# In-projection and pool projection of a hybrid encoder block: token tiles, or feature-major seven-product passes over 1024 tokens

## The chip, the cores and the metric

The kernel runs on one core of a Trainium2 chip. A core has five engines that run side by side and wait for one another by semaphores: TensorE (PE; its weight loads are listed as PEld), VectorE (DVE), ScalarE (ACT), GpSimd (POOL) and SyncE (SP). SP does no arithmetic here: it issues DMA transfers in the order in which the program has them, and an issue that has to wait holds back those behind it. The metric is the device time of the whole kernel in microseconds (us).

## What is computed

One layer of an encoder block over 2048 tokens of width 1024, in float32. Only the first part of it is touched by the change:

```python
xn = rmsnorm(h, g_mix[l])
z = jnp.einsum('bsd,dc->bsc', xn, w_in[l])      # 512 q, 512 k, 512 v, 512 pool columns, 8 gate columns
q = rmsnorm(head_split(q, FOX_HEADS, FOX_HEAD_DIM), g_q_fox[l])     # 8 heads of 64; k alike
fox = forgetting_attention(q, k, v, f_logit)    # causal, with cumulated log-sigmoid gates
pool = multiscale_pool(p_in, w_pool[l], pool_scale[l])  # trailing means over 2, 4, 8, 16 frames, minus the frame, then a map per group
h = h + jnp.einsum('bsc,cd->bsd', jnp.concatenate([fox, pool], axis=-1), w_out[l])
```

Behind it come cross-attention to 256 memory tokens, whose keys and values are a projection of the normed memory, and a gated feed-forward part (FFN). Products have to be nearly as exact as float32.

## The kernel before

**Exactness.** A float32 value is used as a pair: hi is the value rounded to the type fp32r (an ACT copy), lo is what is left (a DVE subtraction, `sub_hi`, L54). `split` (L179) makes the pair, `split_gain` (L175) does so with a factor per partition. A product is then three matmuls (`mm3`, L57): hi by hi, hi by lo and lo by hi. Matmuls on plain float32 data also occur, for small sums; each of them leaves two records in the trace.

**Order.** Where `in_order` is opened, PE and the engines named in it follow the program's order (all of them in the first two stages below, PE alone in the pool stage, PE, DVE and ACT in attention); a planner orders the others by its own costs and by what is ready.

**Stages around the change**, each with its lines:

- Memory keys and values first (L212 to L310): 256 memory tokens by 1024 columns, 96 matmuls of 512 columns, while the in-projection's weights are loaded and split. They go to DRAM (`mkvd`).
- In-projection (L313 to L447): 16 tiles of 128 tokens. For each, the tile of x transposed is the stationary operand, and the 1544 columns of q, k, v and gates are the moving one, in four banks of 386 columns: 4 x 8 x 3 matmuls a tile (`project`, L316). The weights stay on chip as pairs. The row factor of the norm comes from plain float32 sums (`token_sums`, L197) and POOL's `pow` (`rsqrt`, L64), and is applied when a bank is emptied (`scaled`, L324). `normed_heads` (L336) and `split_heads` (L355) norm q and k and split them, `to_heads` (L367) turns them with PE transposes, 16 a tile, to one row per feature, and stores them in DRAM (`qkT`).
- Pool stage (L467 to L628): eight blocks of 256 tokens. `project_p` (L379) has the weights as the stationary operand and 256 columns of x as the moving one, 96 matmuls a block. `windows` (L496) makes the trailing means by doubling sums, all four groups at once; `pooled` (L536) maps them, 12 matmuls a block. `out_sums` (L548) makes weight sums for the output projection on POOL, `cumulated` (L565) the sums of the gates. `load_head` (L456) fetches head 0.
- Attention (from L673): 8 heads by 4 blocks of 512 tokens. `score_items` (L693) issues the scores into `sps`; DVE takes their minima and ACT their exponentials.
- Output projection, cross-attention and FFN. The output projection and the FFN already multiply 2 x 2 blocks of operands with seven products in place of eight: sums and differences of weight blocks are made by DVE or POOL (`weight_ops`, L981; `down_sums`, L1445; `act_sums`, L1466), each block is split, and each product is 12 matmuls of 512 columns into a bank (`product`, L1476). `gate_up` (L1481) is called the gate and up stage below.

## Time and profile before

| what | us |
|---|---|
| median of three timed runs | 2585.02 (2584.59 to 2588.13) |
| the profiled execution, its span from the first to the last instruction | 2586.7 |
| first score of attention issued, in that execution | 460.2 |
| PE busy up to there | 440.13 |

The page gives no other time for the profiled execution than its span, so the span stands for it; it lies 1.7 above the median of the timed runs. In the lines that follow, a row of a timeline has start, length, engine, line of the program, operation, output and inputs, and in brackets how long its engine sat idle before it and what ended that. A row of a group has the number of instructions, their busy time, and the mean length of one in nanoseconds. A row of windows has the window, its length, the busy time of PE, PEld, DVE, ACT and POOL with their numbers of instructions, the granted clock of PE, the DMA share and GB/s.

### The profile page before, as it was taken

The page shows a single profiled execution, that of the slowest core. Times are in us where ns is not written, and L with a number is a line of the kernel's source. Part 1 is how long each engine was busy: PE and PEld are TensorE (multiplying, and loading weights), DVE is VectorE, ACT ScalarE, POOL GpSimd, SP SyncE. Part 2 cuts the span into 40 slices and gives each one's busy share as a digit, 9 for nine tenths or more (in the row PEclk, how much of TensorE's full clock was granted, in tenths as well). Part 3 has the DMA queues.
Part 4 walks back from the last instruction along what each step waited for, and adds up shares of the span by engine and source line. Part 5 has one row for each costly group of instructions (what it writes and reads, how often), then busy time and mean ns, then how long its engine had stood idle before and what let it go on. Part 6 is the DMA issues. An engine that isn't in the chain of part 4 may idle for free.

```text
span 2586.7 us, 37147 instructions
## 1 busy us (share of the span) xinstructions
PE 2522.3 (98%) x13037; PEld 2169.7 (84%) x13037; DVE 1740.9 (67%) x2955; ACT 1286.9 (50%) x2444; POOL 892.2 (34%) x1185
## 2 busy tenths in 40 slices
PE   8999989999999899999999999999999999999998
PEld 7999989788888687788878888888888888888887
DVE  6444477899998755545877778756766666665554
ACT  6454443788889523555643433334543333333443
POOL 3343255445555522344425545430001222222000
PEclk9999999999999999999999999999999999999999
DMA  6443476644543545122464545447773332325665
GB/s 242 127 131 106 127 220 213 175 123 123 152 121 95 171 161 212 70 87 89 177 215 179 187 171 195 147 159 268 247 261 123 113 112 102 127 98 181 230 215 184
DMA packets 223434, 416.13 MB, mean 161 GB/s; under 512 B 26128, under 2 KB 113936, under 8 KB 212496
## 3 DMA queue, kind: packets, MB, share of 16 engines
q1 hardware_dynamic: 190800, 307.84, 37.2%
q0 software_dynamic: 32448, 105.93, 10.6%
q8 instruction: 102, 1.67, 0.3%
q14 instruction: 84, 0.69, 0.1%
HBM read 280.39 MB, written 133.30 MB: 160 GB/s over the span
## 4 chain that ended last, share of the span: by engine, by line
PE 46%; issue 8%; DVE 2%; DMA 2%; ACT 1%; POOL 1%; SPq 0%; POOLq 0%; DVEq 0%; ACTq 0%
PE bk L60 13%; PE bk L62 13%; PE bk L61 13%; PE mmps L60 2%; PE mmps L62 2%; PE mmps L61 2%; PE tp L896 1%; DMA graw<-in_w_gu_dram 1%; DVE ww L55 1%; DVE t L991 0%; DMA xraw<-hTd 0%; POOL out_dram L1578 0%; ACT mq L1069 0%; DMA hTd<-hst 0%; DVE ms L1073 0%
## 5 line engine op out<-in xcount | busy, mean ns | idle before, releaser
L55 DVE TENSOR_TENSOR ww<-draw,ww 128x512 fp32r<-128x512 f32 x308 | 205.3, 703 | 156.5 <-ACT ww L181 155.8
L181 ACT CAST ww<-draw 128x512 fp32r<-128x512 f32 x308 | 179.4, 620 | 219.7 <-PE bk L62 179.2
L55 DVE TENSOR_TENSOR ww<-graw,ww 128x512 fp32r<-128x512 f32 x220 | 179.1, 821 | 107.4 <-ACT ww L181 107.0
L61 PE MATMUL bk<-ww,ww 128*128 128x512 f32 x616 | 239.9, 389 | 0.0
L62 PE MATMUL bk<-ww,ww 128*128 128x512 f32 x616 | 239.8, 389 | 0.0
L60 PE MATMUL bk<-ww,ww 128*128 128x512 f32 x616 | 239.8, 389 | 0.0
L181 ACT CAST ww<-graw 128x512 fp32r<-128x512 f32 x220 | 135.7, 621 | 181.5 <-PE bk L62 158.1
L55 DVE TENSOR_TENSOR pl<-tp,ph 128x512 fp32r<-128x512 f32 (+3 forms) x296 | 176.9, 599 | 27.5 <-ACT ph L809 25.4
L728 ACT ACTIVATE s<-s,mx 128x1024 f32<-128x1024 f32 (+2 forms) x192 | 173.7, 905 | 5.4 <-DVE mx L722 4.5
L793 PE MATMUL tp<-ident,s 128*128 128x128 f32 x1088 | 171.6, 274 | 4.7 <-DVE pl L55 4.3
L60 PE MATMUL zps<-wh,xhi 128*128 128x386 f32 x512 | 175.8, 343 | 0.1
L61 PE MATMUL zps<-wl,xhi 128*128 128x386 f32 x512 | 173.7, 339 | 0.0
L62 PE MATMUL zps<-wh,xl 128*128 128x386 f32 x512 | 173.4, 339 | 0.0
L809 ACT CAST ph<-tp 128x512 fp32r<-128x512 f32 (+3 forms) x296 | 148.5, 513 | 35.9 <-PE tp L793 30.3
L793 PEld LDWEIGHTS tp<-ident,s 128*128 128x128 f32 x1088 | 134.1, 141 | 32.5 <-DVE pl L55 7.7
L1578 POOL DMA_DIRECT2D out_dram<-o x32 | 17.3, 541 | 382.6 <-DVE o L1575 381.6
L62 PE MATMUL bk<-qs,ww 128*128 128x512 f32 x352 | 137.3, 390 | 1.0 <-DVE ww L55 1.0
L60 PE MATMUL bk<-qs,ww 128*128 128x512 f32 x352 | 138.0, 392 | 0.3 <-ACT s L1497 0.3
L61 PE MATMUL bk<-kh,ww 128*128 128x512 f32 x352 | 137.1, 389 | 0.0
L61 PE MATMUL bk<-cb,ww 128*128 128x512 f32 x352 | 137.0, 389 | 0.0
L60 PE MATMUL bk<-kl,ww 128*128 128x512 f32 x352 | 137.0, 389 | 0.0
L62 PE MATMUL bk<-kl,ww 128*128 128x512 f32 x352 | 137.0, 389 | 0.0
(607 smaller groups left out, 7373.4 us busy)
## 6 DMA issues: line engine op xcount, KB each, us to landing
graw<-in_w_gu_dram SPq DMA_DIRECT2D x44, 1024.0 KB, 5.4
draw<-in_w_down_dram SPq DMA_DIRECT2D x66, 256.0 KB, 4.4
xl<-in_xT_dram SPq DMA_DIRECT2D x64, 256.0 KB, 4.9
qkT<-st SPq DMA_DIRECT2D x64, 256.0 KB, 2.7
wdr<-in_w_down_dram SPq DMA_DIRECT2D x22, 512.0 KB, 4.3
vd<-cb SPq DMA_DIRECT2D x16, 512.0 KB, 3.3
qs<-qkT SPq DMA_DIRECT2D x8, 1024.0 KB, 6.8
kh<-qkT SPq DMA_DIRECT2D x16, 512.0 KB, 7.9
```

Source lines behind the costliest of these rows:

```text
L55: (eng or dve).tensor_tensor(out=lo, in0=src, in1=f(hi), op=ALU.subtract)
L60: pe.matmul(ps, lhsT=sh, rhs=mh, start=first, stop=False, skip_group_check=goes_on)
L61: pe.matmul(ps, lhsT=sh, rhs=ml, start=False, stop=False, skip_group_check=goes_on)
L62: pe.matmul(ps, lhsT=sl, rhs=mh, start=False, stop=last, skip_group_check=goes_on)
L181: act.copy(hi, raw)
L728: act.activation(s[:, sl], s[:, sl], AF.Exp, bias=ng, scale=-1.0, accum_out=l[:, q, g:g + 1])
L793: pe.transpose(tp[:, q * P:(q + 1) * P], unit["rows"][q][:, j * P:(j + 1) * P], ident[:])
L809: act.copy(ph[:, sl], tp[:, sl])
L896: pe.transpose(tp[:, e_], src[:, q + e_], ident[:])
L1578: pool.dma_start(out[rows_, cs], o)
```

## The change

The memory stage, the in-projection and the pool stage become one stage, opened with PE and SP in program order and DVE, ACT and POOL left to the planner.

- All 2048 columns of q, k, v and pool are computed with one row per feature, so that the weights are the stationary operand and 512 tokens the moving one. Tokens go in two passes of 1024, features in four groups of 512 (`GROUPS`: pool, q and k of heads 0 to 3, q and k of heads 4 to 7, v). In each group two units of 256 features (u) are multiplied as 2 x 2 blocks: 128 features by 512 input rows, with 512 input rows by 512 tokens. Seven products (o) take the place of eight.
- A step m is one product: 4 x 3 = 12 matmuls of 512 columns into one of the banks a, b and c of its unit. A group has 14 steps (two units, taken in turn), a pass 56, both passes 112. Banks are read between products by ACT copies and DVE additions; a and b go on accumulating after they have been read.
- Weight blocks and their sums (on POOL) are split for every step, six steps ahead (`prep`), into seven places; in each pass all weights are loaded and split again. Sums of x blocks are made once a pass and split (`first_ops`; for the second pass `next_ops` stores them in DRAM and `reload` fetches and splits them).
- The norm's gain is multiplied into x, not into the weights. Its row factor comes from rows of x loaded once more (`row_stats`, ACT squares), and is applied later: in `windows`, in `v_block`, and within the q and k norm as an epsilon times the mean square.
- The eight gate columns are computed apart, with plain float32 matmuls on the x blocks (`forget_block`): 64 for the first 1024 tokens ahead of the product of step 4, and 16 in each of four calls of `next_ops`.
- q and k need no turning. `qk_block` squares the block (ACT), sums over 64 features with plain float32 matmuls, takes `pow` on POOL, stores the factors in DRAM, loads them back spread over the partitions, multiplies, splits and stores. `v_block` turns v with PE transposes, four a block. Pool blocks go to DRAM and come back in `windows`, one group and 512 tokens at a time, in the second pass.
- These jobs are generators: `spawn` enters one at a step, and each `yield` gives the number of steps until it goes on. They share 23 slots of 512 columns on chip and two PSUM banks (`job_bank`).
- Memory keys and values come last, in eight steps of 12 matmuls behind step 111, with their weights split through the same places. Head 0 is loaded at step 104.
- Stores that POOL issued (`poolT`, `osum`) are issued by SP; all transfers of the stage are.
- In attention, two tile pools are opened in the other order, which changes addresses only.

```diff
--- before.py
+++ after.py
...
-                    mm3(kv[m][a][:], (mh[:, ms_], ml[:, ms_]), (wh[:, as_], wl[:, as_]), k == 0, k == KD - 1)
...
-                    mm3(zps[n][:], (hs[k][:, ts], ls[k][:, ts]), (whi[k][:, sl], wlo[k][:, sl]), k == 0, k == KD - 1)
...
-                    mm3(zs[g // per][:, g % per], (wph[k][:, g * P:(g + 1) * P], wpl[k][:, g * P:(g + 1) * P]),
-                        (hs[k], ls[k]), k == 0, k == KD - 1)
...
+    LA = 6
+    WOPS = ("b11", "b21", "t2", "t1", "t3", "t4", "b22")
+    XOPS = ("x11", "x12", "s2", "s1", "s3", "x22", "s4")
+    GSTEPS, PSTEPS = 14, 56
+    LAST = 2 * PSTEPS
+    GROUPS = ("p", "qk0", "qk1", "v")
...
+        t_ = wwi.tile([P, 2, TB], F32R, tag=f"ww{nplace[0] % (LA + 1)}", name="ww", bufs=1)
+        nplace[0] += 1
+        return t_[:, 0], t_[:, 1]
...
+    def prep(m):
...
+        if nm == "t2":
+            t2s[u] = Slot("t2")
+            tt(b11, b12, b11, ALU.subtract, pool)
+            tt(quad(t2s[u].v), b22, b11, ALU.subtract, pool)
+        elif nm == "t1":
+            tt(b12, b22, b12, ALU.subtract, pool)
+        src = {"b11": b11, "b21": b21, "t2": quad(t2s[u].v) if u in t2s else None, "t1": b11, "t3": b12, "t4": b21,
+               "b22": b22}[nm]
+        wops[m] = hi, lo = weight_place()
+        split(quad(hi), quad(lo), src)
+        if nm == "t2":
+            tt(b21, b21, quad(t2s[u].v), ALU.subtract, pool)
+            t2s.pop(u).free()
+    def product(ps, wop, xop, first):
+        for j in range(4):
+            cs = slice(j * P, (j + 1) * P)
+            mm3(ps, (wop[0][:, cs], wop[1][:, cs]), ops[xop][j], first and j == 0, j == 3, not first)
+    def forget_block(T, ks, fps, r, first, last):
+        for n, k in enumerate(ks):
+            pe.matmul(fps, lhsT=r[n], rhs=wf[:, k], start=first and n == 0, stop=last and n == len(ks) - 1)
...
+        for T in range(2):
+            fps = job_bank()[:, :32].rearrange("p (q h) -> p q h", q=4)
+            tiles = [r[nm, j].v for nm in names[2 * T:2 * T + 2] for j in range(4)]
+            for q in range(4):
+                forget_block(T, range(KD), fps[:, q], [t_[:, q * P:(q + 1) * P] for t_ in tiles], True, True)
+            dve.tensor_copy(facc[:, 4 * T:4 * T + 4], fps)
+        for j in range(4):
+            x11, x12, x21, x22 = (r[nm, j].v for nm in names)
+            put("x22", "x22", j)
+            tt(x22, x21, x22, ALU.add)
+            tt(x21, x11, x21, ALU.subtract, pool)
+            tt(x11, x22, x11, ALU.subtract)
+            put("s2", "x11", j)
+            tt(x12, x12, x11, ALU.subtract, pool)
+        for op, nm in (("s1", "x22"), ("s3", "x21"), ("s4", "x12")):
+            for j in range(4):
+                put(op, nm, j)
...
+    def reload(op):
...
+        op_places(op)
+        for j in range(4):
+            split(*ops[op][j], r[j].v)
+            r[j].free()
+            if j == 1:
+                yield 1
...
+    def v_block(m, T, s):
+        yield 3
+        tp = quad(job_bank())
+        for q in range(4):
+            pe.transpose(tp[:, q], s.v[:, q * P:(q + 1) * P], ident[:])
+        s.free()
+        vs = Slot("vs")
+        vq = quad(vs.v)
+        tt(vq, tp, rstd[:, 4 * T:4 * T + 4].unsqueeze(2).to_broadcast([P, 4, P]), ALU.mult)
+        out_ = []
+        for a in range(2):
+            s_ = Slot("vo", F32R)
+            vo = s_.v.rearrange("p (q c d) -> p q c d", q=4, c=2)
+            va = vq[:, :, a * DH:(a + 1) * DH]
+            act.copy(vo[:, :, 0], va)
+            sub_hi(vo[:, :, 1], va, vo[:, :, 0])
+            out_.append(s_)
+        vs.free()
...
+    def qk_block(isk, m, T, s):
+        n = 4 * isk + m
+        sq = Slot("sq")
+        act.activation(sq.v, s.v, AF.Square, scale=0.125)
+        yield 3
+        st = job_bank()[:, :8].rearrange("p (q a) -> p q a", q=4)
+        for q in range(4):
+            pe.matmul(st[:, q], lhsT=sq.v[:, q * P:(q + 1) * P], rhs=bones[:], start=True, stop=True)
+        sq.free()
+        ms = loc1.tile([P, 2, 4], F32, tag="qms", name="qms", bufs=3)
+        r = loc1.tile([P, 2, 4], F32, tag="qr", name="qr", bufs=3)
+        tt(ms[:], st.rearrange("p q a -> p a q"), epsx[:, 4 * T:4 * T + 4].unsqueeze(1).to_broadcast([P, 2, 4]), ALU.add)
+        pool.tensor_tensor(out=r[:].rearrange("p a q -> p (a q)"), in0=ms[:].rearrange("p a q -> p (a q)"),
+                           in1=mhalf[:, :8], op=ALU.pow)
+        yield 2
+        sp.dma_start(rd[n][T].rearrange("a p q -> p a q"), r[:])
+        yield 3
+        rb = Slot("rb")
+        for a in range(2):
+            sp.dma_start(rb.v[a * DH:(a + 1) * DH, :], rd[n][T][a].rearrange("t q -> (t q)").partition_broadcast(DH))
+        yield 2
+        dve.scalar_tensor_tensor(out=quad(s.v), in0=quad(s.v), scalar=gcol[:, isk:isk + 1],
+                                 in1=rb.v.rearrange("p (t q) -> p q t", q=4), op0=ALU.mult, op1=ALU.mult)
+        hi, lo = rb.v.bitcast(F32R), s.v.bitcast(F32R)
+        act.copy(hi, s.v)
+        sub_hi(lo, s.v, hi)
+        yield 2
+        ts = slice(T * TB, (T + 1) * TB)
+        sp.dma_start(qkd[n][0, :, ts], rb.v)
+        sp.dma_start(qkd[n][1, :, ts], s.v)
+        rb.free()
+        s.free()
...
+        rb = rbs[T].v.rearrange("p (t q) -> p q t", q=4)
+        tt(quad(pT[:, HIS:]), quad(pT[:, HIS:]), rb, ALU.mult)
+        if g == NG - 1:
+            rbs.pop(T).free()
+        if T == 0:
+            pool.memset(pT[:, :HIS], 0.0)
+        else:
+            pool.tensor_copy(pT[:, :HIS], tail[:, g])
+        if T < NTB - 1:
+            pool.tensor_copy(tail[:, g], pT[:, TB:])
+        cur = s
+        for st in range(g + 1):
+            sh = 1 << st
+            lead = 2 * sh - 1
+            nx = Slot(f"w{st}")
+            tt(nx.t[:, lead:], cur.t[:, lead:], cur.t[:, lead - sh:HIS + TB - sh], ALU.add, pool if st % 2 else dve)
+            if cur is not s:
+                cur.free()
+            cur = nx
+        if T == 0:
+            fix = loc1.tile([P, HIS], F32, tag="fix", name="fix", bufs=2)
+            tt(fix[:], cur.t[:, HIS:2 * HIS], pinv[:, g], ALU.mult)
+            tt(fix[:], fix[:], pT[:, HIS:2 * HIS], ALU.subtract)
+        mixed = pT[:, HIS:]
+        dve.scalar_tensor_tensor(out=mixed, in0=cur.t[:, HIS:], scalar=1.0 / (2 << g), in1=mixed,
+                                 op0=ALU.mult, op1=ALU.subtract)
+        if T == 0:
+            dve.tensor_copy(pT[:, HIS:2 * HIS], fix[:])
+        cur.free()
+        mh, ml = Slot("mxh", F32R), Slot("mxl", F32R)
+        split(mh.v, ml.v, mixed)
+        s.free()
+        yield 4
+        ps = job_bank()
+        gs = slice(g * P, (g + 1) * P)
+        mm3(ps, (wpool[0].v[:, gs], wpool[1].v[:, gs]), (mh.v, ml.v), True, True)
...
+    with in_order(EN.SP):
+        banks, a0, a1, a2 = {}, {}, {}, {}
+        start = first_ops()
+        next(start)
+        spawn(4, start)
+        for T in range(NTB):
+            spawn((5, 8, 14, 22)[T], row_stats(T))
+            at((15, 18, 50, 50)[T], forget_logits, T)
+        for j in range(4):
+            spawn((8, 17, 25, 34)[j], next_ops(j))
+        for i, op in enumerate(XOPS):
+            spawn(PSTEPS - GSTEPS + 2 + 2 * i, reload(op))
+        spawn(57, pool_weights())
+        for T in range(NTB):
+            t0 = (59, 62, 65, 68), (71, 74, 77, 80), (83, 86, 89, 92), (95, 98, 106, 109)
+            spawn(t0[T][0] - 1, rows_bcast(T))
+            for g in range(NG):
+                spawn(t0[T][g], windows(g, T))
+        for k in range(4):
+            spawn((10, 58, 64, 70)[k], out_sums(k))
+        spawn(70, cumulated())
+        spawn(LAST - 6, mem_tokens())
+        for i in range(8):
+            at(LAST - GSTEPS + (4, 5, 8, 9, 11, 13, 14, 15)[i], load_kv, i)
+        at(LAST - GSTEPS + 6, lambda: head0.extend(load_head(0, hpa)))
+        for m in range(LAST + 8):
+            step[0] = m
+            G, r = divmod(m, GSTEPS)
+            o, u = divmod(r, 2)
+            tick()
+            for u_ in range(2):
+                for kh, lead in enumerate((10, 7)):
+                    n = m + lead - u_
+                    if n % GSTEPS == 0 and 0 < n // GSTEPS < 8:
+                        load_raw(n // GSTEPS, u_, kh)
+            if m + LA < LAST:
+                prep(m + LA)
+            if m < LAST:
+                if o == 0:
+                    for n in "abc":
+                        banks[n, u] = bank(f"{n}{u}")
+                a, b, c = (banks[n, u] for n in "abc")
+                product((a, c, a, b, a, a, b)[o], wops.pop(m), XOPS[o], o in (0, 1, 3))
+                if o == 0:
+                    a0[u] = Slot("a0")
+                    act.copy(a0[u].v, a)
+                elif o == 1:
+                    s = a0.pop(u)
+                    tt(s.v, c, s.v, ALU.add)
+                    block(G, u, 0, 0, s)
+                elif o == 2:
+                    a1[u] = Slot("a1")
+                    act.copy(a1[u].v, a)
+                elif o == 4:
+                    s = Slot("a2")
+                    act.copy(s.v, a)
+                    tt(s.v, b, s.v, ALU.add)
+                    block(G, u, 1, 1, s)
+                elif o == 5:
+                    s = Slot("c21")
+                    act.copy(s.v, a)
+                    block(G, u, 0, 1, s)
+                elif o == 6:
+                    s = a1.pop(u)
+                    tt(s.v, b, s.v, ALU.add)
+                    block(G, u, 1, 0, s)
             else:
+                for n in range(2 * (m - LAST), 2 * (m - LAST) + 2):
+                    kv_item(n)
+                    if n == KD - 1:
+                        spawn(m, mem_keys())
+                if m == LAST + 7:
+                    mem_vals()
+            n = m + LA - LAST
+            for n in (n,) if n < LA else (2 * n - LA, 2 * n - LA + 1):
+                if 0 <= n < 2 * KD:
+                    prep_kv(n)
+        while due:
+            step[0] += 1
+            tick()
+        lstack.close()
+        pstack.close()
+        hp = opened(hps, "hp")
+        v0 = load_values(0)
...
+        tpool = opened(c0, "tpool")
         spool = opened(c0, "spool")
-        tpool = opened(c0, "tpool")
```

More of the change, by code (lines that the diff above doesn't have):

```diff
@@ L96, in block_kernel @@
[L96 to L97 removed]
+    bones = loc1.tile([P, 2], F32, name="bones")
+    pool.memset(bones[:], 0.0)
+    for a in range(2):
+        pool.memset(bones[a * DH:(a + 1) * DH, a:a + 1], 1.0)
     gqm = cst.tile([P, 1], F32, name="gqm")
[L99 to L101 removed]
@@ L114, in block_kernel @@
     B = 256
-    hps = ExitStack()
-    hpa = opened(hps, "hpa")
+    TB = 512
+    NTB = S // TB
     def slab(n, pl=None, dt=F32):
```

810 lines of the change are left out of this document (376 added, 434 removed).

## The prediction

> **What bounds the kernel now.** I read the engine shares first, then the windows of the stages that the change replaces, then single instructions.
>
> ```profile
> span 2586.7 us, 37147 instructions
> PE 2522.3 (98%) x13037; PEld 2169.7 (84%) x13037; DVE 1740.9 (67%) x2955; ACT 1286.9 (50%) x2444; POOL 892.2 (34%) x1185
> ```
>
> ```profile
> 0.00:36.70 36.70, 26.90 (x112) 21.09 (x112) 25.11 (x24) 24.28 (x31) 13.49 (x16) 1.00 0.91 347
> 36.70:335.50 298.80, 298.65 (x1828) 297.27 (x1827) 139.47 (x151) 145.03 (x241) 103.74 (x74) 1.00 0.38 117
> 335.50:460.20 124.70, 114.57 (x912) 111.79 (x911) 99.65 (x160) 47.93 (x90) 64.73 (x96) 0.96 0.74 226
> 460.20:833.00 372.80, 368.53 (x2260) 317.05 (x2258) 346.19 (x1072) 329.70 (x718) 192.44 (x353) 1.00 0.47 134
> ```
>
> ```profile
> L715 PEld LDWEIGHTS sps<-kh,qs x320: 186/188/330, 460.2 to 831.5; 128*128 128x128 f32 x160
> ```
>
> After the window and its length stand busy times of PE, weight load, DVE, ACT and POOL. The four windows are memory keys and values, in-projection, pool stage and attention; the first score is issued at 460.2. Up to there PE is almost always busy while DVE is at 139 of 299 and 100 of 125. So PE binds before, and the first score's moment is what the change can move. Attention behind it is untouched and has DVE at 346 of 373, so a debt of DVE carried into it is hardly worked off there.
>
> The price of a matmul is its distance from the next one (the printed durations overlap):
>
> ```profile
> 229.29 0.34 PE L61 MATMUL zps<-wl,xhi 128*128 128x386 f32 x1
> ...
> 241.64 0.34 PE L62 MATMUL zps<-wh,xl 128*128 128x386 f32 x1
> ```
>
> ```profile
> 337.40 0.28 PE L61 MATMUL zp<-xl,wph 128*128 128x256 f32 x1
> ...
> 345.57 0.28 PE L62 MATMUL zp<-xhi,wpl 128*128 128x256 f32 x1
> ```
>
> ```profile
> 1700.11 0.39 PE L61 MATMUL bk<-x22l,ww 128*128 128x512 f32 x1
> ...
> 1711.89 0.39 PE L62 MATMUL bk<-kl,ww 128*128 128x512 f32 x1
> ```
>
> ```profile
> 228.14 1.02 PE L202 MATMUL ss<-ones,part 128*128 128x1 f32 x8
> 229.02 0.43 PE L60 MATMUL zps<-wh,xhi 128*128 128x386 f32 x1
> ```
>
> ```profile
> 1023.43 0.88 PE tp L896 x8
> ```
>
> 386 columns: 70 steps in 12.35 us, 0.176 each. 256 columns: 70 in 8.17, 0.117. 512 columns: 52 in 11.78, 0.2265. The four plain-f32 products of L202 (two records each) take 0.88, 0.22 each. An f32 transpose takes 0.11.
>
> **The change on PE.** Removed: 1536 products of 386 columns (271 us) and 768 of 256 (90). Added: 112 steps of 12 products of 512 columns, 1344 x 0.2265 = 304.5. That is 56 us less. But the eight gate columns no longer ride in the 386: 128 plain-f32 products (`forget_block`), 28.2. The q and k norms need 128 more (`qk_block`), 28.2. An 8- or 2-column f32 product is not in the trace; the one-column one has 0.22, two 128-column passes (the transpose's 0.11) give the same from above, so 0.22. Values need 64 transposes, with nine others 8.0. Windows: 48 products of 512, 10.9. Memory: 96 of 512 and 16 sums, 21.7 + 3.5; cumulated sums 0.4. Together **405.5 us** of PE before the first score, which comes at 460.2 now. So the new stage may leave PE idle or slow for 54.7 us before it loses.
>
> **Start, 26 us.** The first product now needs four x tiles and a weight quarter, 1.5 MB.
>
> ```profile
> 2.18 0.58 SPq L148 DMA_DIRECT2D xl<-in_memT_dram  x1
> 5.75 0.62 ACT L157 CAST xhi<-xl 128x512 fp32r<-128x512 f32 x1 [3.68 <-DMA xl<-in_memT_dram]
> 10.24 0.63 PE L62 MATMUL kv<-qs,xl 128*128 128x512 f32 x1
> 10.67 0.63 PE L60 MATMUL kv<-qs,xhi 128*128 128x512 f32 x1
> ```
>
> 3.6 us from issue to use, 1.5 MB at the first window's 347 GB/s (4.3), a split (0.62 + 0.69): 9.3. The first twelve products come 0.43 apart rather than 0.23, 2.4. Another 2 for x12 and its weights. Then step 4: PE first does 64 gate products (14 us, in the 405.5), which read x11 to x22 raw, and only then may the sums overwrite them. The step's product needs s2: x22 sum (DVE 0.69), x21 difference (POOL 1.30), x11 (DVE 0.69), copy (ACT 0.62), split (DVE 0.69) and hand-overs, 4.5 us for the first of four tiles, 3.4 for each next (three DVE and one POOL operation that exclude each other, below). The last comes 14.7 after the gates, its products end 0.7 later, against 2.7 without a wait: 12.7. Bounds of this stall: 4.5 (later tiles keep PE's pace) and 16.6 (POOL does the x12 difference between, 4.7 a tile). Sum 26.4.
>
> **The middle: DVE beside POOL.** Here I chose. Rows of timeline, then groups of the window 1320 to 1560 (gate and up, the same weight sums and splits):
>
> ```profile
> 13.44 1.30 POOL L162 TENSOR_TENSOR part<-part,xsq 128x512 f32<-128x512 f32 x1 [1.16 <-ACT xsq L160]
> 13.49 1.80 DVE L55 TENSOR_TENSOR xl<-xl,xhi 128x512 fp32r<-128x512 f32 x1
> ```
>
> ```profile
> 58.63 3.35 POOL L71 TENSOR_TENSOR zrq<-zms,mhalf 128x16 f32<-128x16 f32 x1
> 60.23 0.69 DVE L55 TENSOR_TENSOR xl<-xl,xhi 128x512 fp32r<-128x512 f32 x1 [0.25 <-ACT xhi L157]
> ```
>
> ```profile
> L55 DVE TENSOR_TENSOR ww<-graw,ww 128x512 fp32r<-128x512 f32 x62 | 60.3, 983 | 29.6 <-ACT ww L181 29.4
> L1473 POOL TENSOR_TENSOR s<-s,s 128x512 f32<-128x512 f32 x23 | 29.9, 1302 | 0.4
> L55 DVE TENSOR_TENSOR ww<-t,ww 128x512 fp32r<-128x512 f32 x25 | 25.7, 1034 | 2.9 <-ACT ww L181 2.9
> L1449 POOL TENSOR_TENSOR wdr<-wdr 128x512 f32<-128x512 f32 x18 | 25.3, 1406 | 0.7
> L991 DVE TENSOR_TENSOR t<-graw 128x512 f32<-128x512 f32 x14 | 20.6, 1469 | 8.4 <-DMA graw<-in_w_gu_dram 8.4
> L991 DVE TENSOR_TENSOR graw<-graw 128x512 f32<-128x512 f32 x13 | 16.5, 1270 | 0.0
> L991 DVE TENSOR_TENSOR t<-graw,t 128x512 f32<-128x512 f32 x13 | 14.8, 1135 | 0.3
> L1449 POOL TENSOR_TENSOR t<-wdr 128x512 f32<-128x512 f32 x6 | 9.1, 1509 | 6.1 <-DVE s L1514 6.0
> L1514 DVE TENSOR_TENSOR s<-bk,s 128x512 f32<-128x512 f32 x13 | 8.9, 686 | 1.6 <-issue 0.8 <-PE bk L62 0.8
> ```
>
> ```profile
> 227.43 0.74 DVE L177 SCALAR_TENSOR_TENSOR wpl<-wpr,colt,wph 128x512 fp32r<-128x512 f32 x1
> 439.59 0.42 DVE L521 SCALAR_TENSOR_TENSOR mixed<-s,pT 128x256 f32<-128x256 f32 x1
> ```
>
> A DVE subtraction takes 0.69, but 1.80 when a POOL sum has begun 0.05 before it; the `pow` of L71 does not hold it. The five slow DVE groups have 62 x 0.29 + 25 x 0.34 + 14 x 0.78 + 13 x 0.58 + 13 x 0.44 = 51 us over 0.69, for 47 POOL sums: **about 1.05 us of DVE per POOL sum**. Bounds: 0 (a sum lies beside bank reads, which at 686 are not held) and 1.40 (the whole L1449 sum).
>
> [...]
>
> A step is 2.72 us, a group of 14 is 38.1. Each group has 14 weight splits and 6 bank sums, 20 x 0.69 = 13.8 of DVE, and 8 POOL sums. On top, by the steps at which jobs run (a q/k block's late pair 0.74 + 0.69 = 1.43; a v block 0.69 and two halves of 0.42, 1.53; a window four or five operations, 2.8 or 3.5):
>
> - steps 42 to 55: six q/k pairs 8.6, four to five v blocks 6.9, 20 reload splits 13.8, small 0.8: DVE 43.9, POOL 8 sums, PE 40.2
> - 56 to 69: v blocks 5.4, eight reload splits 5.5, three windows and edge fixes 10.3, pool weights 0.7: 35.7, 18 sums (out_sums has eight), PE 41.1
> - 70 to 83: q/k 4.1, five windows 16.5, cumulated sums 1.6: 36.0, 21 sums (15 tiny carries counted as three), PE 49.1
> - 84 to 97: q/k 12.7, four windows 12.6: 39.1, 12 sums, PE 47.8
> - 98 to 111: eight weight and six memory splits, bank sums 14.1, q/k 8.6, v 6.9, windows 9.1, memory tokens 2.8: 41.5, 4 sums, PE 42.1
>
> DVE 196.2 + 63 x 1.05 = 262.4 against PE 220.3: **42 us** over. ACT's copies, one of 0.62 for each split, bank and square, are some 400, 250 us in all, and hide beside PE; without that cover they would be late like DVE's. Before step 42 PE has the larger sum (steps 28 to 41: DVE 44, PE 52). The last eight steps have DVE 22 of 28 us and give 6 back. PE feels the debt soon: bank b, read by DVE behind o = 4, is needed again three steps later, and a job bank after about two. So 36.
>
> **Queues.** All stores, POOL's too, now go through SP, some 460 issues of at most 0.58 us (the row above) in over 400 us. A q/k block's `rd` store waits there for POOL's `pow`, and weight and window loads stand behind it; raw weights are loaded three to four steps ahead of their splits, which covers a POOL lag of 8 us. I add nothing. The memory loads at the end share DMA with head 0 (4 MB); attention then finds head 0 loaded, as now. `tpool` before `spool` changes places alone.
>
> **Sum.** 405.5 + 26 + 36 = 467.5, the first score 7.3 us later than 460.2; the rest is unchanged. The profiled execution's span of 2586.7 becomes 2594; the median of the runs, 2585.0, lies 1.7 under that span, so **2592**.
>
> **Rivals.** *Faster:* DVE's debt never reaches PE, because sums fall beside bank reads and ACT's copies. It decides at 24.1 / 63 = 0.38 us per sum; below that the 36 go, the first score comes at 432 and the time is 2556. For it: the pool stage ran POOL at 65 and DVE at 100 of 125 with PE at 115. Against: 1.05 where POOL sums were sparser than here. *Much slower:* each sum holds DVE 1.40 (88 us, debt 64, less 6) and the s2 chain takes its upper bound: 405.5 + 30 + 58, 33 us later, 2618. For it: both engines are full in steps 56 to 83. *No saving on PE:* products of 512 in this order keep less than the FFN's pace; nothing in the trace speaks for it.
>
> **How the numbers follow.** Forecast case (2580 to 2605) 0.45, faster rival 0.32, much slower 0.18, others 0.05. Within 0.2% (5.2 us, about what a measurement of this kernel tells from no change) lies part of the forecast case, 0.16; faster 0.36 with its lower edge, slower 0.48. The range leaves out the ends of both rivals: 2553 to 2620.
>
> **What would show it.** The first score by `sps`: 467 (432, 494). A PE gap of some 13 us behind the gate products at about 36 us. In steps 42 to 111 DVE busy over 95%, its two-input operations at a mean near 1.0 us, and PE waits on DVE of weight splits or bank sums. If DVE is under 85% there, the forecast is wrong towards faster; if PE waits on DMA, the queue paragraph is wrong.

## The result and the profile after

The changed kernel takes 2711.42 us (median of four runs, 2707.98 to 2714.1) against 2586.57 for the kernel before: 1.0472 times as long, with a 95% interval of 1.0451 to 1.0493. The forecast was 2592, in a range of 2553 to 2620. Slower was right; the size was 125 us where 7 were expected. The profiled execution took 2713.41 us and has a span of 2711.7. Two rows of the page, then the first weight load of the scores, whose first start is the mark that the prediction named:

```profile
span 2711.7 us, 36599 instructions
PE 2564.6 (95%) x12293; PEld 2130.6 (79%) x12293; DVE 1854.8 (68%) x3165; ACT 1306.8 (48%) x2539; POOL 962.1 (35%) x1222
```

```profile
L871 PEld LDWEIGHTS sps<-kh,qs x320: 186/188/337, 578.3 to 952.0; 128*128 128x128 f32 x160
```

The first score comes at 578.3, not at 460.2 (before) or 467 (forecast). So 118.1 of the span's 125.0 us arise ahead of it. Behind it 6.9 more are lost, most of them in the output projection; that is about the spread of the four runs and was not followed up.

The time up to the first score as windows, of the kernel before and of the changed one (window and length, then busy time of PE, weight load, DVE, ACT and POOL with the count of instructions, the granted PE clock, the DMA share, GB/s):

```profile
0.00:460.20 460.20, 440.13 (x2847) 430.14 (x2848) 264.23 (x335) 217.23 (x361) 181.96 (x186) 0.99 0.52 165
```

```profile
0.00:578.30 578.30, 475.99 (x2109) 390.00 (x2109) 378.71 (x546) 239.07 (x460) 252.33 (x225) 0.86 0.67 200
```

The 2109 matmul records, each at the price that the prediction gave its kind, make 405.3 us. The forecast of the work was 405.5. But PE was busy for 475.99 on it, 70.7 more, and idle for 102.3. The clock column says why busy time grew: 0.86 of full speed where it had been 0.99. PE was given half its clock for a good part of the stage.

The same in four stretches: steps 0 to 13, 14 to 41, 42 to 111, and the memory keys and values behind them.

```profile
0.00:108.10 108.10, 78.84 (x328) 65.70 (x329) 67.49 (x82) 40.82 (x81) 53.05 (x46) 0.76 0.50 163
108.10:225.10 117.00, 111.18 (x538) 93.88 (x536) 56.65 (x102) 48.49 (x104) 44.54 (x38) 0.90 0.70 212
225.10:523.30 298.20, 250.40 (x1088) 200.84 (x1088) 218.03 (x306) 124.68 (x229) 143.71 (x125) 0.90 0.69 198
523.30:578.30 55.00, 35.57 (x159) 29.56 (x158) 36.54 (x58) 25.08 (x48) 11.02 (x18) 0.78 0.77 251
```

| stretch | length | PE work at the prices | PE idle | PE slow (busy less work) | lost | forecast of the loss |
|---|---|---|---|---|---|---|
| steps 0-13 | 108.1 | 55.7 | 29.3 | 23.1 | 52.4 | 26 |
| steps 14-41 | 117.0 | 98.1 | 5.8 | 13.1 | 18.9 | 0 |
| steps 42-111 | 298.2 | 222.3 | 47.8 | 28.1 | 75.9 | 36 |
| memory | 55.0 | 29.3 | 19.4 | 6.3 | 25.7 | 0 |

The reader is to see two things. The loss is everywhere, not in one place. And in the third stretch DVE, which the prediction had as the bound at over 95%, is busy for 218 of 298 us, 73%: PE waited, and no engine was full.

Where the clock went first: the gate products of the start, and a window inside them.

```profile
32.23 24.05 PE L286 MATMUL jb<-wf,x 128*128 128x8 f32 x128
```

```profile
36.00:56.00 20.00, 20.00 (x96) 20.00 (x95) 0.85 (x3) 0.00 (x0) 0.00 (x0) 0.50 0.15 55
```

PE goes from one product to the next for 24.05 us without a pause. Its clock is at 1.00 for the first 3.6 us (32.2 to 35.8) and at half from there on: 0.188 us a record on average where 0.11 was priced. From 36 to 56 DVE is busy for 0.85 us, and ACT and POOL not at all, since the sums have to wait until the raw tiles are read.

And how PE came to wait in the middle. Timeline rows around one gap, by engine (start, length, engine, line, operation; in brackets the idle time before it and who ended it):

```profile
331.36 1.26 DVE L210 TENSOR_TENSOR fix<-w,rowt 128x16 f32<-128x16 f32 x1 [1.24 <-POOL pT L529]
332.65 1.19 DVE L210 TENSOR_TENSOR fix<-fix,pT 128x16 f32<-128x16 f32 x1
333.87 1.70 DVE L548 SCALAR_TENSOR_TENSOR pT<-w,pT 128x512 f32<-128x512 f32 x1
335.61 1.11 DVE L551 COPY pT<-fix 128x16 f32<-128x16 f32 x1
```

```profile
331.32 1.26 POOL L210 TENSOR_TENSOR raw<-raw 128x512 f32<-128x512 f32 x1
332.55 4.15 POOL L210 TENSOR_TENSOR wo<-wo 128x512 f32<-128x512 f32 x3
```

```profile
336.80 0.62 ACT L149 CAST mxh<-pT 128x512 fp32r<-128x512 f32 x1 [11.13 <-issue]
337.33 0.61 ACT L149 CAST ww<-raw 128x512 fp32r<-128x512 f32 x1
337.85 0.58 ACT L766 COPY a<-a 128x512 f32<-128x512 f32 x1
```

```profile
338.48 0.80 PE L60 MATMUL a<-x22h,ww 128*128 128x512 f32 x1 [8.48 <-ACT a L766]
339.07 0.63 PE L61 MATMUL a<-x22l,ww 128*128 128x512 f32 x1
339.49 0.63 PE L62 MATMUL a<-x22h,ww 128*128 128x512 f32 x1
339.92 0.63 PE L60 MATMUL a<-x22h,ww 128*128 128x512 f32 x1
```

From the last fence upwards: PE waits 8.48 us for ACT's copy of bank `a`. That copy needs nothing any more; it stands in ACT's queue behind the cast of a pool window, for which ACT idles 11.13 us. (The row of that cast names no releaser; DVE's copy into the window ends at 336.72, 0.08 before it.) The window is late because, last of all, four DVE operations take 5.3 us, three of them of 16 columns, each about as long as the POOL sum beside it. The same four for another window, nine microseconds earlier and with no POOL sum beside them, take 1.2:

```profile
322.09 0.18 DVE L210 TENSOR_TENSOR fix<-w,rowt 128x16 f32<-128x16 f32 x1
322.30 0.17 DVE L210 TENSOR_TENSOR fix<-fix,pT 128x16 f32<-128x16 f32 x1
322.59 0.69 DVE L548 SCALAR_TENSOR_TENSOR pT<-w,pT 128x512 f32<-128x512 f32 x1
...
323.31 0.17 DVE L551 COPY pT<-fix 128x16 f32<-128x16 f32 x1
```

So a held operation on DVE costs not only its own length but can cost that of a queue behind it, on another engine. The gap costs clock as well: the products behind it come 0.43 apart, not 0.23.

### The profile page after: what moved, and what is told of

Its sections match the earlier page's. It is cut to its first block, busy times and chain, and to the rows that moved or that the text cites. A ratio compares the mean times of both kernels' runs of the same rounds, so it can differ in the third digit from the quotient of the medians.

```text
span 2711.7 us, 36599 instructions
## 1 busy us (share of the span) xinstructions
PE 2564.6 (95%) x12293; PEld 2130.6 (79%) x12293; DVE 1854.8 (68%) x3165; ACT 1306.8 (48%) x2539; POOL 962.1 (35%) x1222
## 4 chain that ended last, share of the span: by engine, by line
PE 45%; issue 8%; DVE 2%; DMA 1%; ACT 1%; POOL 1%; SPq 0%; POOLq 0%; DVEq 0%; ACTq 0%
PE bk L62 13%; PE bk L61 13%; PE bk L60 13%; PE mmps L60 2%; PE mmps L62 2%; PE mmps L61 2%; PE tp L1052 1%; DMA xraw<-hTd 0%; DMA wqr<-in_w_mem_q_dram 0%; DVE ww L55 0%; POOL out_dram L1734 0%; DMA hTd<-hst 0%; ACT mq L1225 0%; DVE ms L1229 0%; PE mops L60 0%
## 5 line engine op out<-in xcount | busy, mean ns | idle before, releaser
L965 ACT CAST ph<-tp 128x512 fp32r<-128x512 f32 (+3 forms) x296 | 148.8, 514 | 39.9 <-PE tp L949 34.3
L149 ACT CAST ww<-t 128x512 fp32r<-128x512 f32 x104 | 64.6, 622 | 171.4 <-PE bk L62 129.3
L934 PE MATMUL acc<-ph,v 128*128 128x512 f32 (+1 forms) x320 | 133.9, 423 | 2.9 <-POOL ph L954 2.9
L61 PEld LDWEIGHTS bk<-ww,ww 128*128 128x128 f32 x616 | 115.6, 188 | 25.3 <-DVE ww L55 1.2
```

The lines of the kernel that those rows point to most:

```text
L61: pe.matmul(ps, lhsT=sh, rhs=ml, start=False, stop=False, skip_group_check=goes_on)
L149: act.copy(hi, raw)
L934: pe.matmul(acc[:, qa * P:], lhsT=v[:, j, :], rhs=pm[:, qa * P:], start=state["n"] == 1, stop=state["n"] == 2 * nk)
L965: act.copy(ph[:, sl], tp[:, sl])
```

## Experiments

Three theories are used in the expectations. **L** is the prediction's: POOL sums hold DVE. **Q**: ACT and DVE work through a fixed order in which PE's bank copies and weight splits stand behind job operations that still wait. **C**: the run of gate products costs PE its clock and holds up the start. The measure is the first score, since from there to the end all kernels need 2124 to 2135 us. The four runs of the changed kernel lie 6 us apart; smaller differences are not read. All kernels but the last were timed once, so a difference of 10 to 13 us rests as much on the rows shown with it as on its size. In e8 the instructions of every engine keep the order of the changed kernel. In the others the planner sets the order anew, and what that alone is worth was not separated.

| kernel | edit | first score | against 578.3 | time |
|---|---|---|---|---|
| e1_no_rows | q/k rows not read back | 543.0 | -35.3 | 2678.0 |
| e8_contig | rows read without stride | 567.8 | -10.5 | 2701.0 |
| f4_dve_rows | e6, rows through POOL's queue | 545.4 | -32.9 | 2682.1 |
| e2_no_pool | no POOL sums | 522.5 | -55.8 | 2654.8 |
| e5_shadow | POOL sums that nobody reads | 582.3 | +4.0 | 2717.8 |
| e6_on_dve | sums on DVE | 532.7 | -45.6 | 2668.3 |
| e4_few_gates | 88 of 128 gate products left out | 547.6 | -30.7 | 2676.1 |
| g1_swap | gates feature-major | 542.7 | -35.6 | 2676.9 |
| f1_start | start in another order | 567.0 | -11.3 | 2700.1 |
| e3_inorder | program order on ACT, DVE, POOL | 656.7 | +78.4 | 2788.1 |
| f2_memq | memory load through POOL's queue | 588.3 | +10.0 | 2717.0 |
| e7_all_three | e1, e2 and e4 together | 459.8 | -118.5 | 2585.1 |
| f5_dve_swap | e6 and g1 | 506.3 | -72.0 | 2634.1 |
| f6_start | f5, start in another order | 501.8 | -76.5 | 2633.7 |

### The POOL sums

**e2_no_pool**

```diff
-            tt(b11, b12, b11, ALU.subtract, pool)
-            tt(quad(t2s[u].v), b22, b11, ALU.subtract, pool)
...
         for st in range(g + 1):
+            if st % 2:
+                continue
...
-        tt(r[0].v, b12, b11, ALU.subtract, pool)
```

> Left out: POOL's weight sums, its sums of the output weights and its window sums (81 sums of 128x512 from step 0 on), their readers take the raw tiles. Theory L: each of these held DVE about 1.05 us and DVE is the bound in the middle, so steps 42 to 111 shorten by 45 to 65 us and the first score comes at 515 to 535. Theory Q: only the waits that hang on a POOL result go (weight splits on t, window chains), 10 to 30 us; first score 548 to 568, with gaps behind q/k rows still there.

The trace counts 96 such sums in the changed kernel, not 81: 64 of weights, 16 of output weights, 16 of windows. First score 522.5, inside L's range and outside Q's. But leaving out a sum takes away its result as well, and its readers no longer wait for it. So:

**e5_shadow**

```diff
-            t2s[u] = Slot("t2")
-            tt(b11, b12, b11, ALU.subtract, pool)
-            tt(quad(t2s[u].v), b22, b11, ALU.subtract, pool)
+            shd = Slot("t2")
+            tt(quad(shd.v), b12, b11, ALU.subtract, pool)
+            tt(quad(shd.v), b22, b11, ALU.subtract, pool)
+            tt(quad(shd.v), b21, b22, ALU.subtract, pool)
+            shd.free()
```

> As the kernel without POOL sums (first score 522.5), but POOL makes as many sums of the same tiles at the same places into a spare slot that nobody reads; the weight sums, window sums and output-weight sums are thus still left out of the result. If a POOL sum costs because it holds DVE (theory L), the 55.8 us come back: first score 560 to 580, and DVE's two-input operations again take 1.1 to 1.9 beside them. If it costs because weight splits and windows wait for its result (theory Q), the first score stays at 520 to 535.

First score 582.3, 2.3 above L's range: all of the gain is gone again, with sums whose results nobody reads. The steps 42 to 111 of e2 and of e5, each with DVE's largest group there, the weight splits (836 ns in the changed kernel):

```profile
212.10:467.20 255.10, 237.45 (x1088) 192.49 (x1088) 183.76 (x305) 124.19 (x226) 55.20 (x63) 0.95 0.81 232
```

```profile
L55 DVE TENSOR_TENSOR ww<-raw,ww 128x512 fp32r<-128x512 f32 x66 | 45.2, 688 | 11.3 <-ACT ww L149 11.0
```

```profile
226.70:529.80 303.10, 254.57 (x1089) 204.27 (x1088) 229.22 (x305) 122.90 (x226) 149.26 (x129) 0.89 0.67 196
```

```profile
L55 DVE TENSOR_TENSOR ww<-raw,ww 128x512 fp32r<-128x512 f32 x66 | 59.7, 911 | 14.6 <-ACT ww L149 14.5
```

The 305 DVE instructions take 183.76 us without sums and 229.22 beside them, PE's clock falls from 0.95 to 0.89, and the stretch is 48.0 us longer. That the sums hold DVE is shown, and that the cost comes back without any reader of their results. The edit is not quite free of waits: by the profile, ACT waits in a few places for a sum to leave its spare slot, longest at 360.52 (12.56 us) and 418.91 (6.96). At the first of these DVE's held window ended at the same moment, so PE would have stood still there all the same; for the others that was not settled. The hold is 45.5 us for 66 POOL instructions more, 0.69 each; against the changed kernel itself (218.03 of DVE, 125 POOL instructions, in the row above) it is 34.3 us for 62, 0.55 each.

**e6_on_dve**

```diff
-            tt(b12, b22, b12, ALU.subtract, pool)
+            tt(b12, b22, b12, ALU.subtract)
...
-            tt(nx.t[:, lead:], cur.t[:, lead:], cur.t[:, lead - sh:HIS + TB - sh], ALU.add, pool if st % 2 else dve)
+            tt(nx.t[:, lead:], cur.t[:, lead:], cur.t[:, lead - sh:HIS + TB - sh], ALU.add)
```

> Nothing left out: the same sums (those of the start too) run on DVE, not on POOL. Theory L at 1.05 us of DVE for each POOL sum against 0.69 for a DVE operation: DVE busy in steps 42 to 111 falls a little or stays near 218, hand-overs to POOL go, first score 15 to 40 us earlier than 578. If DVE's own work is what is short, it gets no earlier: 575 to 600.

First score 532.7, 45.6 earlier, more than L's 15 to 40. 10.6 of it lie in the steps 0 to 13. Most of that is not due to the sums of x, for e2, which leaves those on POOL, gains 9.5 there; in both, the 4.8 us that PE waits at 23.7 for a weight split are gone. DVE has 104 instructions more up to the first score and is busy for 380.9 us, where it was 378.7: what it does itself it no longer loses to the hold. Hand-overs to POOL go as well, and the two were not separated.

### The gate products

**e4_few_gates**

```diff
-        for n, k in enumerate(ks):
-            pe.matmul(fps, lhsT=r[n], rhs=wf[:, k], start=first and n == 0, stop=last and n == len(ks) - 1)
+        pe.matmul(fps, lhsT=r[0], rhs=wf[:, ks[0]], start=True, stop=True)
```

> Left out: 88 of the 128 gate products (one product of each group of eight or two stays). Theory C (the run of 64 eight-column products drops PE to half clock, 24.05 us where 14.1 were priced, and everything of the start stands behind it): the start shortens by 21 us, the later ones by 7, and less of the following products is at half clock: first score 28 to 36 us earlier. If a gate product cost only the priced 0.22: 88 x 0.22, 19 us earlier.

30.7 us earlier, 11.3 more than the products' own price. This is C's range, but fewer products also leave less work. The next kernel keeps all of them:

**g1_swap**

```diff
-                forget_block(T, range(KD), fps[:, q], [t_[:, q * P:(q + 1) * P] for t_ in tiles], True, True)
+        g = [gates_wide(range(KD), [r[nm, j].v for nm in names[2 * T:2 * T + 2] for j in range(4)]) for T in range(2)]
...
+            pe.matmul(ps, lhsT=wf[:, k], rhs=tiles[n], start=n == 0, stop=n == len(ks) - 1)
+        act.copy(g.v[:H], ps)
...
+            pe.transpose(fps[:, q], g.v[:H, q * P:(q + 1) * P], ident[:H, :H])
```

> Nothing left out: the gates are made feature-major, 8 gate columns as the stationary side and 512 tokens moving (32 plain f32 products of 512 columns), then turned in 64 transposes of 8x128. Same place, same tiles read. If the clock halves because the run of 8-column products keeps the array nearly idle, the granted clock stays near 1.0 between 36 and 56 us, the first 64 products' stretch of 24.05 becomes 14 to 18 and the first score comes 8 to 16 us earlier than 578. If it halves for another reason, the stretch lasts as long or longer and the first score stays at 574 to 590. No row has the price of an f32 product of 512 columns; four passes of 0.2265 would make 0.91.

The same gates of the start, and a window inside them:

```profile
31.57 13.90 PE L287 MATMUL jb<-x,wf 128*8 128x512 f32 x32
```

```profile
32.00:45.00 13.00, 13.00 (x32) 2.70 (x30) 6.31 (x11) 4.39 (x9) 3.81 (x3) 1.00 0.43 144
```

13.90 us, not 24.05, for the same sums over the same tiles, and the clock stays at 1.00. A plain-f32 product of 512 columns costs 0.87 (two records of 0.434), or 3.84 times the 0.2265 of a matmul of as many columns on fp32r data; the expectation's estimate had four times. The first score is 35.6 us earlier, more than C's 8 to 16, since the 64 later gate products and the products around them lose less too: steps 14 to 55 lose 20 where they lost 42.2. What halved the clock is a long run of products of this shape, shown by changing the shape alone. Whether it is the eight columns, or the load of 128 stationary columns that each of these products brings along, is not separated: PEld is busy for 20.00 of 20 us in the window of the changed kernel, for 2.70 of 13 here.

**f1_start**

```diff
+        for j in range(4):
+            tt(raw[j][0], xs[j][2], xs[j][3], ALU.add)
+            tt(raw[j][1], raw[j][0], xs[j][0], ALU.subtract)
+            split(*ops["s2"][j], raw[j][1])
...
+        for T in (1, 0):
...
+                if q % 2:
+                    yield 1
```

> Nothing left out: at the start the sums s1 and s2 are made first, into the place that s4 takes later, and the 64 gate products follow in four runs of 16 between the steps 5 to 8, so no product waits for the run of gates and no run is longer than 3.6 us. The s2 product of step 4 starts near 40, not 61.8; if a long run of small products is what halves the clock, the gate products stay near 0.11 us a record. First score 22 to 32 us earlier. If the clock halves at any gate product, 14 to 20 us.

11.3 us earlier, below both ranges. The s2 product did start at 36.25, not 61.76. Two of the four runs of gates:

```profile
43.90 6.83 PE L286 MATMUL jb<-wf,x 128*128 128x8 f32 x32
...
55.64 3.95 PE L286 MATMUL jb<-wf,x 128*128 128x8 f32 x32
```

The second runs at close to full clock (0.12 us a record), but the 512-column products behind it come 0.43 apart. The first finds the clock at half already (0.50 in the window 44 to 51): PE had waited 4.11 us for the s2 product, and that product's matmuls come 0.43 apart too, as do those behind the run. So even a run of 3.95 us left the clock down, and spreading narrow products among wide ones passed it on to the wide ones. The expectation had counted only the gates.

### The q and k rows

**e1_no_rows**

```diff
-        for a in range(2):
-            sp.dma_start(rb.v[a * DH:(a + 1) * DH, :], rd[n][T][a].rearrange("t q -> (t q)").partition_broadcast(DH))
...
-                                 in1=rb.v.rearrange("p (t q) -> p q t", q=4), op0=ALU.mult, op1=ALU.mult)
+                                 in1=ident[:].unsqueeze(1).to_broadcast([P, 4, P]), op0=ALU.mult, op1=ALU.mult)
```

> Left out: the q and k norm rows are not read back from DRAM, q and k are multiplied with the identity tile instead. Same matmuls, casts, subtractions and POOL sums, 64 loads fewer. Theory Q (queue order: ACT and DVE work in a fixed order in which the bank copies and weight splits that PE needs stand behind job operations that still wait, for the q/k row above all): the ACT waits on DVE's L480 (43.1 + 16.2 us in the changed kernel) go, and with them PE gaps of 6.8, 7.0 and part of 8.5 in the middle; first score 15 to 35 us earlier than 578. Theory L (the prediction's: POOL sums hold DVE, which is the bound): DVE and POOL have the same work, so the first score stays within 5 us of 578.

First score 543.0, at Q's edge. The steps 42 to 55 fall from 66.3 to 46.0 us, and the 17.24 us that PE waits ahead of the memory tokens' sums become 6.91. But the edit did more than take a wait away. The operation that uses the row, in the changed kernel and here (least, median and most ns):

```profile
L480 DVE SCALAR_TENSOR_TENSOR a<-a,gcol,rb x24: 1109/1144/2209, 163.7 to 536.1; 128x512 f32<-128x512 f32 x24
```

```profile
L480 DVE SCALAR_TENSOR_TENSOR a<-a,gcol,ident x24: 731/741/1820, 120.5 to 459.8; 128x512 f32<-128x512 f32 x24
```

It reads the row at a stride of four elements and takes 1.14 us, not the 0.74 that the prediction took from an unstrided row. And in the changed kernel DVE waited for a row itself only 3.6 us in all. So:

**e8_contig**

```diff
-                                 in1=rb.v.rearrange("p (t q) -> p q t", q=4), op0=ALU.mult, op1=ALU.mult)
+                                 in1=quad(rb.v), op0=ALU.mult, op1=ALU.mult)
```

> Changed in the result alone: q and k are multiplied with the row read in the order in which it lies, so with factors of the wrong tokens. Every instruction, load, wait and queue order stays; only DVE's operation of L480 no longer reads one input at a stride of four elements (1.14 us in the changed kernel, 0.74 where the identity tile stood in). Theory S (the 35.3 us of the rows are, for the greater part, DVE's longer operation, 32 x 0.40 = 13 us on an engine that holds up bank sums and casts): first score 10 to 20 us earlier than 578.3. Theory R (they are the round trip through DRAM and where the planner puts the readers): within 5 us of 578.3.

10.5 us earlier with L480 at a median of 0.746 (1.144 in the changed kernel) and the same order on every engine: S at its lower edge. The 32 operations are 12.7 us shorter in all, so the stride is about 10 of the 35.3.

**f4_dve_rows**

```diff
-        sp.dma_start(rd[n][T].rearrange("a p q -> p a q"), r[:])
+        pool.dma_start(rd[n][T].rearrange("a p q -> p a q"), r[:])
...
-            sp.dma_start(rb.v[a * DH:(a + 1) * DH, :], rd[n][T][a].rearrange("t q -> (t q)").partition_broadcast(DH))
+            pool.dma_start(rb.v[a * DH:(a + 1) * DH, :], rd[n][T][a].rearrange("t q -> (t q)").partition_broadcast(DH))
```

> Nothing left out: the sums run on DVE as in the kernel with first score 532.7, and the q and k rows are stored and read back through POOL's queue, where they stand right behind POOL's own power, not through SP's behind weight and window loads. If the 35.3 us of the rows come from SP's queue, first score 505 to 522. If they come from the DRAM round trip itself or from where the planner puts the readers, 528 to 545.

545.4, at the upper end of the second range and 12.7 later than the kernel that it changes (532.7). DVE now waits for rows, 51.6 us in all; the largest group of these waits (us in total, times, longest):

```profile
DVE a L480 <- DMA rb<-rd5t: 16.8, 3, 9.3
```

Freed of SP's weight and window loads, the rows came later, behind what POOL waits for. SP's queue is not shown to be the cause. What the other 25 us or so of the rows are, the round trip, the slots that it keeps or the place that the planner then gives the readers, stays open.

### The order of the queues

**e3_inorder**

```diff
-    with in_order(EN.SP):
+    with in_order(EN.SP, EN.Activation, EN.DVE, EN.Pool):
```

> Nothing left out: ACT, DVE and POOL take their instructions of the stage in the order in which the program writes them, not in the planner's. Each bank copy then stands ahead of the jobs of the next step. Theory Q: PE waits on bank copies (24.6 us) and on sq and mxh (19.3 us) shrink, first score 20 to 60 us earlier, unless program order puts other waiting operations ahead. Theory L: the same operations exclude each other, first score within 10 us of 578.

78.4 us later: Q's promise failed, by the exception that it named. The first product alone is 21 us late. In the order as written DVE's first operation waits for a constant that is loaded behind the x tiles, and the gains of x stand behind it:

```profile
24.72 0.15 DVE L100 TENSOR_SCALAR gcol<-gcol 128x1 f32<-128x1 f32 x1 [24.72 <-DMA gcol<-in_rows_dram]
```

```profile
31.86 0.80 PE L60 MATMUL a<-qs,ww 128*128 128x512 f32 x1 [31.86 <-ACT ww L149]
```

The order matters much, but the planner's was better than the written one.

**f2_memq**

```diff
-        sp.dma_start(raw, memT.rearrange("(k p) m -> p k m", p=P))
+        pool.dma_start(raw, memT.rearrange("(k p) m -> p k m", p=P))
```

> Nothing left out: the memory tokens are loaded through POOL's queue, not SP's, where the load stood behind a window load until 524.9. Theory Q: the tokens are there some 10 us earlier and PE's gap of 17.2 us ahead of the token sums shrinks to 5 to 9; first score 8 to 12 us earlier, 566 to 570. If the gap is DVE's late value blocks that hold both job banks, it stays: 575 to 579.

The gap ahead of the token sums shrinks from 17.24 to 10.54, as expected, yet the first score is 10.0 later:

```profile
518.64 0.63 ACT L647 ACTIVATE kh<-qs 128x512 f32<-128x512 f32 x1 [12.54 <-DMA qs<-in_memT_dram]
...
523.05 0.56 ACT L766 COPY a<-a 128x512 f32<-128x512 f32 x1
```

```profile
523.67 0.79 PE L60 MATMUL a<-x22h,ww 128*128 128x512 f32 x1 [9.70 <-ACT a L766]
```

With the load issued earlier the planner put the squares of the tokens ahead of two bank copies. The data came later than planned, ACT stood still for 12.54 us, and PE waited 9.70 for a copy whose bank was long full. This is Q's mechanism, made by an edit.

### Together

**e7_all_three** is e1, e2 and e4 in one kernel.

> Left out together what three earlier kernels left out one at a time: the rows read back for q and k (-35.3), 96 POOL sums of weights and windows (-55.8) and 88 gate products (-30.7). If the three are separate causes their gains add up to 121.8 and the first score comes at 456, near the 460.2 of the kernel before; if two of them repair the same wait, later than 475. PE work is then 386.0, so 70 us of idle and half clock stay in the first case, and they have other causes.

```profile
0.00:459.80 459.80, 416.72 (x1934) 339.31 (x1934) 313.42 (x546) 239.30 (x460) 120.20 (x129) 0.94 0.76 235
```

459.8: 118.5 of the 121.8 add up, so the three are separate. That this is as much as the 118.1 us by which the first score had come later is chance: the kernel also leaves out 19 us of priced PE work, and of PE's idle 102.3 us 43.1 are left, of the 70.7 slow ones 30.7. Even so the stage is no shorter than the one it replaces (460.2).

**f5_dve_swap** is e6 and g1, **f6_start** adds to it a start in which s1 and s2 are made beside the gate products:

```diff
+        raw_ = [xo.tile([P, S], F32, tag="s4" + c, name="sr" + c, bufs=1) for c in "hl"]
...
+        for j in range(4):
+            tt(raw[j][0], xs[j][2], xs[j][3], ALU.add)
+            tt(raw[j][1], raw[j][0], xs[j][0], ALU.subtract)
+            split(*ops["s2"][j], raw[j][1])
```

> Nothing left out: sums on DVE (-45.6 alone) and feature-major gates (-35.6 alone) together. If they are separate causes, first score 490 to 505; if the second repairs what the first has repaired, 510 to 530.

> Nothing left out: as the kernel with sums on DVE and feature-major gates, and at the start s1 and s2 are made in the place that s4 takes later, so that DVE makes them beside the 14 us of gate products and not behind them. The wait of the s2 product on ACT and DVE behind the gates (11 to 13 us in the changed kernel) goes: first score 8 to 14 us earlier than that kernel's, about 485, and a time near 2618, still slower than before.

f5 comes at 506.3, 72.0 of 81.2 us and 1 us above its range: nearly separate. f6 comes at 501.8; its start is 7.1 shorter, but 5.1 are given back in the steps 28 to 41, so the 4.5 left miss the 8 to 14 and are less than the runs tell apart.

```profile
0.00:501.80 501.80, 445.06 (x1957) 342.77 (x1957) 380.83 (x650) 244.50 (x470) 113.35 (x121) 0.95 0.77 230
```

f6 is the fastest kernel here that computes everything: 2633.65 us (2631.57 to 2636.78, four runs), 1.0178 times the kernel before (1.0160 to 1.0196). That is 77.8 us better than the changed kernel and still slower than before. No version that computes everything was found to be as fast as the kernel before.

## Why the prediction was wrong in size

- **PE's work, 405.5 us: right** in count and price (405.3). But the prices were taken at full clock (at 0.50, behind the gap at 338, products of 512 columns came 0.43 apart where 0.2265 was priced), and the sum took full clock for granted outside the first twelve products. 70.7 us went there, where 2.4 were summed: the largest miss. With feature-major gates (g1) 45.6 are left; of these, some stand behind waits, like the products behind the gap at 338, and the rest was not traced.
- **Start, 26 us: 52.4.** Its waits were about right: idle 29.3, where 9.3 + 2 + 12.7 = 24.0 were summed; the four gaps of the s2 chain make 13.2 for 12.7. What failed is "64 gate products (14 us, in the 405.5)". They took 24.05 and left the clock down, 23.1 us slow where 2.4 were summed. The price came from rows in which such products were few.
- **Middle, 36 us: 75.9.** The POOL term was nearly right, by luck: leaving the sums out shortens the steps 42 to 111 by 43.1 us (298.2 to 255.1), and 42 was the debt. Its working was not. A sum holds DVE 0.55 to 0.69 us, not 1.05, the weight splits run at 836 ns, and DVE was busy 73%, not over 95%. The prediction balanced each engine's busy time against PE's. In the gap at 338 a held operation made ACT's queue wait, and PE with it, while every engine had time to spare over the stretch. For that reason its test "if DVE is under 85% there, the forecast is wrong towards faster" pointed the wrong way.
- **"Queues. I add nothing": failed.** 35.3 us hang on the q and k rows: about 10 on a strided read priced at 0.74 (1.14), the rest unsettled. The memory stage, also at nothing, lost 25.7, with 17.24 in one wait. The working looked at which DMA stands behind which in SP's queue, and not at which bank copy stands behind which cast in ACT's.
- **Steps 14 to 41, at nothing: 18.9,** 13.1 of it slow clock; with feature-major gates about 3 in all.
- **"The rest is unchanged": 6.9 us off,** about the spread of the runs.
- **The rivals.** "Faster" lost, though its point of decision, 0.38 us a sum, was close to the 0.55 measured. "Much slower" had the right sign but a cap of 33 us, since it too knew only busy sums. The prediction gave slower 0.48 and expected 7 us, so that slower came true is in good part luck.

## What to carry to other kernels

When four in-order engines pass tiles to each other, do not add busy times only: for each operation that PE waits for, name what stands ahead of it in its own queue and what that in turn waits for (8.48 us of PE in the gap at 338). Price matmuls with the clock that their own shape will get: count narrow ones as able to halve it, for themselves and for what follows (here, eight columns wide: 24.05 us for the 13.90 of g1, and in f1 0.43 for 0.23 in the products behind). And an earlier load can make things worse (10.0 us in f2), because an order planned around it puts its readers ahead of work that was ready.

## What the runs showed of the hardware

- A run of f32 matmuls with 8 moving columns lost half of PE's clock without any pause: 24.05 us, from 3.6 us on at 0.50, against 13.90 at 1.00 for the same gates with 512 moving columns.
- A DVE operation with one input at a stride of four f32 elements took 1.14 us, unstrided 0.74 to 0.75.
- POOL sums held DVE operations of 16 columns as well as those of 512: 1.1 to 1.3 us each for 16 columns beside sums of 1.3 to 1.4, and 0.17 to 0.18 with no sum beside them; 1.70 for 512 columns, and 0.69 with none. The hold goes the other way too: in the kernel before, a POOL sum that began at 15.52, 0.30 us into a DVE operation of 1.27, took 2.12, and the one at 13.44, which began ahead of its DVE neighbour, 1.30.
